# Down-projection weight operands of 5 and 7 of 11 chunk pairs made beside the gate and up products and kept in DRAM

## Chip, cores and metric

The kernel runs on one core of one Trainium2 chip. The metric is the device time of one execution in microseconds; the median of three runs is used. The engines are TensorE (PE), VectorE (DVE), ScalarE (ACT), GpSimd (POOL) and SyncE (SP), which issues all transfers.

## What is computed

Two layers of a decoder trunk on 1024 tokens of 1024 features, in f32. Each has a mixer (three head groups with one input and one output projection) and a feed-forward part; each part is scaled and gated by rows that are made from a condition vector `c`:

```python
for l in range(DEPTH):                       # DEPTH = 2
    mod = (c_act @ ada_w[l] + ada_b[l])[:, None, :]
    sh1, sc1, g1, sh2, sc2, g2 = jnp.split(mod, N_MOD, axis=-1)
    ...                                      # mixer, x = x + g1 * (y @ w_out[l])
    h = rms_norm(x, norm2_w[l]) * (1.0 + sc2) + sh2
    gate, up = jnp.split(h @ w_gate_up[l], 2, axis=-1)
    x = x + g2 * ((jax.nn.silu(gate) * up) @ w_down[l])
return rms_norm(x, final_norm_w)
```

The hidden size of the feed-forward part is 2816: 22 chunks of 128, taken as 11 pairs.

## The kernel before

**Products.** Every f32 product is three matmuls on values split in a high and a low part (`mm3`, lines 132 to 134: high x high, low x high, high x low in some order). `split` (lines 139 to 141) makes the parts: ScalarE casts the high part (L140), VectorE subtracts it from the source for the low part (L137, in the helper `sub`). Gate, up and down products use Winograd's form of Strassen's identity: seven block products in place of eight. The generators `left` and `right` give the operands of the seven products in order, with additions and subtractions of blocks in between, on the engine that their caller names.

**Stages of the feed-forward part.** First the gate and up products, pair by pair (`gu_pair`, `pair_steps`, 11 pairs, 7 products each of 24 matmuls). Their weights are loaded as `gur` (four loads of 0.5 MB a pair), combined on POOL (L1406) and split into `gus`. ScalarE and VectorE take the results out of PSUM (the tiles p1, u2, u4, s12; copies at L1477, L1491, L1496); the activated pairs go to DRAM as `act`. In layer 0 the rows of modulation for later are made beside it (`ada_bg`: one load `ada` of 0.5 MB and one VectorE multiply-add, L254, per product).

Then the down products. The 11 pairs are in four groups (`GROUPS`: pairs 0 to 2, 3 and 4, 5 to 7, 8 to 10). `dn_load` reads the activations (`act`) and the down weights (`dnr`, two tiles of 128x1024 a pair). `dn_prep` multiplies the weights by the gate row g2 (`g2row`, L1531; one tile on VectorE, `GE0`, the other on POOL, `GE1`), builds the left operands from the activations and the right ones from the weights, both with four additions or subtractions of 128x512 on POOL (`DNE`, L1406), and splits both: `dns` (left) and `dnt` (right). `dn_group` makes the seven products of a group: 4 token tiles x 3 (or 2) pairs x 3 matmuls each, and after each token tile VectorE adds the PSUM bank to the residual x (L1556).

**What sets the order.** The program is written as steps; the framework's scheduler then gives each engine one fixed order, which the engine runs through without overtaking. `ahead` in `pair_steps` runs one step of the background work per product and makes operands up to `AHEAD` products ahead; in the down stage `want_dn(7 * gi + i + 2)` makes operands one product ahead of the running one. Buffers are of 4 KB a partition: pool G (`NG` = 30), pool W (`NW` = 12: gus, dns, dnt, ada and the sums acc), pool R (4: gur and the first pair of a group), AD (`NAD` = 3 of 2 KB: differences). A tile waits until the buffer that it takes is released. All transfers stand in one order on SP.

Of the kernel before, what the change touches and what calls it, by code (L numbers as in the profile page):

```python
# [68 lines left out]
NG = 30  # L69
# [3 lines left out]
NAD = 3  # L73
# [3 lines left out]
def tile_trunk(ctx, tc, x, c, positions, ada_w, ada_b, norm1_w, w_in, a_sinks, b_q_norm_w, b_w_uq,  # L77
# [19 lines left out]
    def psum_banks(singles, pairs):  # L97
        """open the PSUM pools of a phase: single banks, and pairs of banks."""
# [77 lines left out]
    # ---- silu(c), features on partitions  # L176
# [17 lines left out]
    def sequences(seqs):  # L194
        """named sequences of steps: run one step of a sequence, or as many as are needed."""
# [25 lines left out]
    # layer 0: the first norm's shift and scale as columns, summed over features by VectorE and TensorE,  # L221
    # applied to normalised tokens that are transposed already
# [34 lines left out]
    def load_ada0(hf):  # L257
        """column half of the rows of shift and scale, loads in the order of use."""
# [41 lines left out]
    def after(dst, src):  # L300
        """the load into dst starts once src is there."""
        DVE.tensor_copy(out=dst[0:1, 0:1], in_=src[0:1, 0:1])

    def setup_rest(late):
        # ---- per-feature vectors: rows in, one transpose, columns out
# [21 lines left out]
        # ---- rotary tables, token-major  # L327
# [23 lines left out]
    def rope(q, nh, half, t, f0):  # L351
        """q: view [P, nh, 2, half] in SBUF, rotated in place."""
# [9 lines left out]
    # ---- adaLN modulation  # L362
# [8 lines left out]
    GE1 = POOL  # L371
    cqd = [[dr.tile([P, 384], F32, name=f"cq{l}_{t}") for t in range(NT)] for l in range(DEPTH)]
# [22 lines left out]
    def ada_rows_wide(l, js):  # L395
        """the same with whole rows at a time, loads one step ahead; five steps per row."""
# [32 lines left out]
    def ada_bg(todo):  # L429
        """the same beside the feed-forward layer, rows (layer, index); nine steps per row."""  # L430
# [27 lines left out]
    # ---- building blocks  # L458
    def transpose_tile(xn):
        """two views [P, 4, P] in PSUM: features on partitions."""  # L460
# [8 lines left out]
    def load_in_chunk(l, c0, n, per, late=None):  # L469
        """in-projection weights [1024, n] at column c0: per-k (hi, lo); generator, fills its list."""  # L470
# [53 lines left out]
    def group_rstd(sq, n, dst):  # L524
        """1/rms over 384 features on partitions; sq(k, i): squares of k-th 128 features, tokens i."""
# [8 lines left out]
    def layer(l, x_tiles):  # L534
# [10 lines left out]
        # -- in-projection: a_v | c_q first, then q | k beside the window attention, c_kv | k_rope, u | v  # L545
# [93 lines left out]
        if l == 0:  # L639
            # the steps of the start, in the order of PRS; each first runs the steps that it needs.  The norm and the  # L640
# [521 lines left out]
        def b_av(h, Q, prs, sm):  # L1162
# [53 lines left out]

            return gen_t(), gen_m()

        # -- output projection, gate folded into its weights
        X = {}  # L1220
        yT = {}

# [498 lines left out]
```

## Time and profile before

| | us |
|---|---|
| median of 3 runs | 2422.22 (2413.93 to 2423.72) |
| span of the profiled execution, first to last instruction | 2416.1 |
| TensorE busy in it | 2270.5 |
| VectorE busy in it | 1783.5 |
| ScalarE busy in it | 1096.1 |
| POOL busy in it | 1088.8 |

The time of the profiled execution as a whole is not among the three runs; only its span is known. TensorE's busy time counts matmuls that are pipelined, so it says when TensorE had work, not how fast it went; the number of matmuls that start in a stretch says that. The rows below are of that execution. "dnt<-dnr" names the written and the read tile without buffer numbers; SPq is SP's order of transfers.

### The profile page before, as it was taken

The page shows a single profiled execution, that of the slowest core. Times are in us where ns is not written, and L with a number is a line of the kernel's source. Part 1 is how long each engine was busy: PE and PEld are TensorE (multiplying, and loading weights), DVE is VectorE, ACT ScalarE, POOL GpSimd, SP SyncE. Part 2 cuts the span into 40 slices and gives each one's busy share as a digit, 9 for nine tenths or more (in the row PEclk, how much of TensorE's full clock was granted, in tenths as well). Part 3 has the DMA queues.
Part 4 walks back from the last instruction along what each step waited for, and adds up shares of the span by engine and source line. Part 5 has one row for each costly group of instructions (what it writes and reads, how often), then busy time and mean ns, then how long its engine had stood idle before and what let it go on. Part 6 is the DMA issues. An engine that isn't in the chain of part 4 may idle for free. (4 is left out here: it accounts for less than half of the span.)

```text
span 2416.1 us, 31750 instructions
## 1 busy us (share of the span) xinstructions
PE 2270.5 (94%) x11195; PEld 1909.4 (79%) x11195; DVE 1783.5 (74%) x2743; ACT 1096.1 (45%) x2244; POOL 1088.8 (45%) x1055
## 2 busy tenths in 40 slices
PE   5999899998999999888899999999899999999897
PEld 4789798887888888776778889888788888887676
DVE  7786678769676667999974854886784444489998
ACT  4566478535333333333344654772553333333333
POOL 4766630243323233856644655112543231375764
PEclk9999999999999999999999999999999999999999
DMA  6403522313454546630140032133223222273111
GB/s 250 163 19 124 169 94 97 127 53 106 156 183 143 167 149 227 225 114 32 32 155 22 21 111 105 53 106 114 78 75 101 79 79 93 69 284 143 36 35 70
DMA packets 133859, 269.01 MB, mean 111 GB/s; under 512 B 10154, under 2 KB 69316, under 8 KB 133700
## 3 DMA queue, kind: packets, MB, share of 16 engines
q1 hardware_dynamic: 133700, 266.99, 32.4%
q8 instruction: 88, 1.44, 0.2%
q14 instruction: 71, 0.58, 0.1%
HBM read 212.38 MB, written 54.57 MB: 110 GB/s over the span
## 5 line engine op out<-in xcount | busy, mean ns | idle before, releaser
L137 DVE TENSOR_TENSOR gus<-gur,gus 128x512 fp32r<-128x512 f32 x264 | 237.9, 914 | 134.4 <-ACT gus L140 133.2
L1406 POOL TENSOR_TENSOR gur<-gur 128x512 f32<-128x512 f32 x44 | 64.1, 1456 | 501.9 <-DVE gus L137 500.9
L140 ACT CAST gus<-gur 128x512 fp32r<-128x512 f32 x264 | 162.4, 622 | 279.0 <-PE gate L134 105.6
L132 PE MATMUL down<-dnt,dns 128*128 128x512 f32 x616 | 248.8, 404 | 38.2 <-DVE x L1556 33.6
L133 PE MATMUL down<-dnt,dns 128*128 128x512 f32 x616 | 248.4, 403 | 15.4 <-DVE dnt L137 15.4
L134 PE MATMUL down<-dnt,dns 128*128 128x512 f32 x616 | 246.4, 400 | 0.0
L133 PE MATMUL gate<-hTl,gus 128*128 128x512 f32 x616 | 240.3, 390 | 4.0 <-DVE hTl L137 4.0
L132 PE MATMUL gate<-hTh,gus 128*128 128x512 f32 x616 | 241.6, 392 | 2.5 <-ACT u L1496 1.3
L132 PE MATMUL up<-hTh,gus 128*128 128x512 f32 x616 | 241.5, 392 | 2.1 <-ACT u L1491 2.1
L134 PE MATMUL up<-hTh,gus 128*128 128x512 f32 x616 | 241.0, 391 | 0.0
L133 PE MATMUL up<-hTl,gus 128*128 128x512 f32 x616 | 241.0, 391 | 0.0
L134 PE MATMUL gate<-hTh,gus 128*128 128x512 f32 x616 | 239.9, 389 | 0.0
L140 ACT CAST dns<-act 128x512 fp32r<-128x512 f32 x132 | 81.7, 619 | 256.3 <-PE down L134 184.6
L132 PEld LDWEIGHTS down<-dnt,dns 128*128 128x128 f32 x616 | 120.3, 195 | 67.7 <-issue 29.1
L133 PEld LDWEIGHTS down<-dnt,dns 128*128 128x128 f32 x616 | 120.5, 196 | 45.1 <-DVE dnt L137 20.1
L1556 DVE TENSOR_TENSOR x<-x,down 128x512 f32<-128x512 f32 x224 | 146.6, 675 | 6.6 <-PE down L134 6.6
L137 DVE TENSOR_TENSOR dnt<-dnr,dnt 128x512 fp32r<-128x512 f32 x132 | 149.7, 1134 | 1.7 <-ACT dnt L140 1.6
L137 DVE TENSOR_TENSOR dns<-act,dns 128x512 fp32r<-128x512 f32 x132 | 136.8, 1036 | 6.8 <-ACT dns L140 6.5
L134 PEld LDWEIGHTS down<-dnt,dns 128*128 128x128 f32 x616 | 120.1, 195 | 25.5
L133 PEld LDWEIGHTS gate<-hTl,gus 128*128 128x128 f32 x616 | 115.8, 188 | 29.0 <-DVE hTl L137 5.6
L132 PEld LDWEIGHTS gate<-hTh,gus 128*128 128x128 f32 x616 | 115.6, 188 | 28.5 <-ACT u L1496 1.7
L132 PEld LDWEIGHTS up<-hTh,gus 128*128 128x128 f32 x616 | 116.8, 190 | 26.7 <-ACT u L1491 2.5
(400 smaller groups left out, 6192.3 us busy)
## 6 DMA issues: line engine op xcount, KB each, us to landing
gur<-in_w_gate_up_dram SPq DMA_DIRECT2D x88, 512.0 KB
ada<-in_ada_w_dram SPq DMA_DIRECT2D x80, 512.0 KB
act<-act SPq DMA_DIRECT2D x44, 512.0 KB
dnr<-in_w_down_dram SPq DMA_DIRECT2D x44, 512.0 KB
wr<-in_w_in_dram SPq DMA_DIRECT2D x24, 512.0 KB
act<-u SPq DMA_DIRECT2D x44, 256.0 KB
x<-in_x_dram SPq DMA_DIRECT2D x16, 512.0 KB
ada0w<-in_ada_w_dram SPq DMA_DIRECT2D x16, 512.0 KB
```

What stands on the lines that cost most here:

```text
L132: PE.matmul(ps, lh, rh, start=start, stop=False, skip_group_check=more)
L133: PE.matmul(ps, lh, rl, start=False, stop=False, skip_group_check=more)
L134: PE.matmul(ps, ll, rh, start=False, stop=stop, skip_group_check=more)
L137: eng.tensor_tensor(out=out_, in0=a, in1=b, op=ALU.subtract)
L140: ACT.copy(out=h, in_=src)
L1406: return lambda o, a, b, op: eng.tensor_tensor(out=o, in0=a, in1=b, op=op)
L1556: DVE.tensor_tensor(out=av_, in0=av_, in1=ps[t], op=ALU.add)
```

## The change

Some pairs are early: 0, 1, 3, 5, 8 in layer 0 and 0, 1, 3, 5, 6, 8, 9 in layer 1. For these the right operands of the down products (weights times g2, the four subtractions, the seven splits) are made by a second background generator, `wd_early`, one step per gate and up product from the second pair on, after 10 steps in layer 0 and 1 in layer 1. Eight steps make a pair. The subtractions are on VectorE there, the multiplication on VectorE and POOL as before. The seven operands of a pair take turns in pool W (`wpe`) and are written to DRAM (`wpd`, 0.5 MB each). In the down stage `dn_prep` reads them back into `dnt` for early pairs, in place of weights, multiplication, subtractions and splits; the left operands are made as before. The row g2 is loaded once, early. NG becomes 33, NAD 4, and a scratch size given to the compiler is made smaller. Comments that the new file leaves out are not shown.

```diff
+EARLY = ((0, 1, 3, 5, 8), (0, 1, 3, 5, 6, 8, 9))
+EARLY0 = (10, 1)
-NG = 30
+NG = 33
-NAD = 3
+NAD = 4
...
+    wpd = [{j: [dr.tile([P, 2, 512], F32, name=f"wp{l}_{j}_{i}") for i in range(7)] for j in EARLY[l]}
+           for l in range(DEPTH)]
...
         def dn_load(grp):
             for j in grp:
                 A = R if j == grp[0] else G
-                r.append([f(2 * j + m, A) for f in (load_act, load_wd) for m in range(2)])
+                r.append((j, [f(2 * j + m, A) for f in ((load_act,) if j in EARLY[l] else (load_act, load_wd))
+                              for m in range(2)]))
...
+        def wd_early():
+            for _ in range(EARLY0[l]):
+                yield
+            g2.append(mod_row(l, 5))
+            for j in EARLY[l]:
+                ws = [load_wd(2 * j + m, G) for m in range(2)]
+                yield
+                for w, E in zip(ws, (GE0, GE1)):
+                    E.tensor_tensor(out=w, in0=w, in1=g2[0], op=ALU.mult)
+                last = None
+                for i, src in enumerate(right(ws[0][:, :512], ws[0][:, 512:], ws[1][:, :512], ws[1][:, 512:],
+                                              AD("t2"), tt_on(DVE))):
+                    v = W([P, 2, 512], F32R, "wpe")
+                    split(src, v[:, 0], v[:, 1])
+                    if last is not None:
+                        DMA.dma_start(out=wpd[l][j][i - 1], in_=f32(last))
+                    last = v
+                    if i < 6:
+                        yield
+                yield
+                DMA.dma_start(out=wpd[l][j][6], in_=f32(last))
...
         def dn_prep(raws):
...
-            for _ in range(7):
+            for i in range(7):
                 ops = []
-                for gl, gr in gens:
+                for j, gl, gr in gens:
+                    v = W([P, 2, 512], F32R, "dnt")
+                    if gr is None:
+                        DMA.dma_start(out=f32(v), in_=wpd[l][j][i])
                     w = W([P, 2, 512], F32R, "dns")
                     split(next(gl), w[:, 0], w[:, 1])
-                    v = W([P, 2, 512], F32R, "dnt")
-                    split(next(gr), v[:, 0], v[:, 1])
+                    if gr is not None:
+                        split(next(gr), v[:, 0], v[:, 1])
...
                 if j > 0:
                     run(bg)
+                    run(bg2)
...
+        bg2 = wd_early()
         for j in range(1, NJ):
             drain(pair_steps(j))
         drain(bg)
+        drain(bg2)
...
-        g2row = mod_row(l, 5)
...
-    nc = _bacc.Bacc("TRN2", target_bir_lowering=False, num_devices=1)
+    nc = _bacc.Bacc("TRN2", target_bir_lowering=False, num_devices=1, dynamic_dma_scratch_size=1024)
```

TensorE's order is the same in both kernels. On the other engines it shows at three places. The first is VectorE in the last group (pairs 8 to 10) of layer 0's down stage, one product. Before:

```order
L1556 TENSOR_TENSOR x_9452<-x_9452,down_10778 128x512
L1556 TENSOR_TENSOR x_9454<-x_9454,down_10779 128x512
L1556 TENSOR_TENSOR x_9456<-x_9456,down_10780 128x512
L137 TENSOR_TENSOR dns_11040<-act_10368,dns_11040 128x512
L137 TENSOR_TENSOR dnt_11044<-dnr_10372,dnt_11044 128x512
L1556 TENSOR_TENSOR x_9458<-x_9458,down_10781 128x512
L137 TENSOR_TENSOR dns_11047<-act_10376,dns_11047 128x512
L137 TENSOR_TENSOR dnt_11051<-dnr_10380,dnt_11051 128x512
L137 TENSOR_TENSOR dns_11054<-act_10384,dns_11054 128x512
L137 TENSOR_TENSOR dnt_11058<-dnr_10388,dnt_11058 128x512
```

And after the change:

```order
L1590 TENSOR_TENSOR x_9723<-x_9723,down_10977 128x512
L1590 TENSOR_TENSOR x_9725<-x_9725,down_10978 128x512
L1590 TENSOR_TENSOR x_9727<-x_9727,down_10979 128x512
L139 TENSOR_TENSOR dns_11294<-act_10584,dns_11294 128x512
L139 TENSOR_TENSOR dns_11298<-act_10588,dns_11298 128x512
L1590 TENSOR_TENSOR x_9729<-x_9729,down_10980 128x512
L139 TENSOR_TENSOR dnt_11297<-dnr_10592,dnt_11297 128x512
L139 TENSOR_TENSOR dns_11305<-act_10596,dns_11305 128x512
L139 TENSOR_TENSOR dnt_11304<-dnr_10600,dnt_11304 128x512
```

One subtraction of ten operations is gone, that of the early pair 8. The second place is SP's order of transfers in layer 0's gate and up stage, around the loads `gur` of the sixth pair. Before:

```order
L1472 DMA act_7_222<-u_1512_7268 128x512
L1426 DMA gur_7508<-in_w_gate_up_dram 128x4x256
L1426 DMA gur_7510<-in_w_gate_up_dram 128x4x256
L435 DMA ada_7505<-in_ada_w_dram 128x1024
L1426 DMA gur_7512<-in_w_gate_up_dram 128x4x256
L1426 DMA gur_7514<-in_w_gate_up_dram 128x4x256
L1472 DMA act_8_223<-p_1524_7386 128x512
```

And after the change (`wp_1_3` is the fourth operand of pair 1 in DRAM):

```order
L1476 DMA act_7_222<-u_1523_7392 128x512
L439 DMA ada_7612<-in_ada_w_dram 128x1024
L1550 DMA wp_1_3_269<-wpe_7577 128x1024
L1550 DMA wp_1_4_270<-wpe_7615 128x1024
L1430 DMA gur_7666<-in_w_gate_up_dram 128x4x256
L439 DMA ada_7659<-in_ada_w_dram 128x1024
L1430 DMA gur_7668<-in_w_gate_up_dram 128x4x256
L1430 DMA gur_7670<-in_w_gate_up_dram 128x4x256
L1476 DMA act_8_223<-p_1540_7525 128x512
L1430 DMA gur_7672<-in_w_gate_up_dram 128x4x256
L1550 DMA wp_1_5_271<-wpe_7662 128x1024
L1516 DMA dnr_7775<-in_w_down_dram 128x1024
```

Three stores and a load of down weights stand between and behind the gate loads. The third place is ScalarE at the same point of the program. Before:

```order
L140 CAST gus_7527<-gur_7512 128x512
L140 CAST gus_7530<-gur_7510 128x512
L140 CAST gus_7533<-gur_7514 128x512
L1491 COPY u_1555_7568<-gate_7387 128x512
L140 CAST gus_7538<-gur_7508 128x512
L1491 COPY u_1556_7570<-up_7388 128x512
```

And after the change:

```order
L142 CAST wpe_7662<-dnr_7413 128x512
L142 CAST gus_7674<-gur_7334 128x512
L142 CAST gus_7677<-gur_7338 128x512
L142 CAST gus_7682<-gur_7666 128x512
L142 CAST gus_7685<-gur_7670 128x512
L142 CAST gus_7688<-gur_7668 128x512
L1495 COPY u_1575_7726<-gate_7526 128x512
L142 CAST gus_7691<-gur_7672 128x512
L142 CAST gus_7696<-gur_7666 128x512
L1495 COPY u_1576_7728<-up_7527 128x512
```

The cast of an early operand has come in ahead, and a cast of `gus` has moved from before the first copy of `u` to behind it, where it takes the buffer that the store wp_1_5 releases.

## Rows read from the trace of the kernel before

**Rows 1.** Page, part 1: busy us, share of the span, instructions.

```profile
PE 2270.5 (94%) x11195; PEld 1909.4 (79%) x11195; DVE 1783.5 (74%) x2743; ACT 1096.1 (45%) x2244; POOL 1088.8 (45%) x1055
```

**Rows 2.** Tile down, each layer: ns min/median/max, first to last start in us.

```profile
L132 PE MATMUL down<-dnt,dns x308: 387/389/767, 984.2 to 1234.2; 128*128 128x512 f32 x154
...
L132 PE MATMUL down<-dnt,dns x308: 387/389/793, 2160.4 to 2406.3; 128*128 128x512 f32 x154
```

**Rows 3.** Timeline of PE, layer 0's down stage, first and last of 42 rows: start, us.

```profile
1140.66 0.39 PE L132 MATMUL down<-dnt,dns 128*128 128x512 f32 x1
...
1149.95 0.39 PE L134 MATMUL down<-dnt,dns 128*128 128x512 f32 x1
```

**Rows 4.** Windows of ten us, layer 0's down stage; x counts what started.

```profile
core 0: us, PE busy (x) PEld busy (x) DVE busy (x) ACT busy (x) POOL busy (x), PEclk, DMA share, GB/s
...
994.00:1004.00 10.00, 8.73 (x39) 6.94 (x38) 10.00 (x9) 2.75 (x5) 9.92 (x7) 1.00 1.00 391
1004.00:1014.00 10.00, 7.86 (x34) 5.89 (x33) 10.00 (x8) 4.37 (x8) 9.92 (x5) 1.00 0.60 240
1014.00:1024.00 10.00, 7.59 (x22) 5.63 (x22) 10.00 (x12) 0.00 (x0) 1.88 (x1) 0.66 0.12 43
1024.00:1034.00 10.00, 10.00 (x46) 8.26 (x45) 10.00 (x16) 3.72 (x7) 1.83 (x1) 1.00 0.75 274
...
1114.00:1124.00 10.00, 6.23 (x28) 4.82 (x26) 10.00 (x9) 3.74 (x7) 10.00 (x7) 1.00 0.00 1
...
1134.00:1144.00 10.00, 10.00 (x46) 8.29 (x45) 8.86 (x15) 4.97 (x10) 0.00 (x0) 1.00 0.35 107
```

**Rows 5.** Waits of PE in layer 0's down stage: us in total, times, longest.

```profile
PE down L132 <- DVE x L1556: 16.8, 4, 6.0
PE down L133 <- DVE dnt L137: 10.9, 7, 2.4
```

**Rows 6.** Timeline of POOL and DVE, layer 0's down stage: start, us, operation.

```profile
1007.48 8.39 POOL L1531 TENSOR_TENSOR dnr<-dnr,mrow 128x1024 f32<-128x1024 f32 x3
...
1010.79 2.87 DVE L137 TENSOR_TENSOR dnt<-t,dnt 128x512 fp32r<-128x512 f32 x1
...
1022.22 0.68 DVE L137 TENSOR_TENSOR dnt<-dnr,dnt 128x512 fp32r<-128x512 f32 x1
```

**Rows 7.** Groups by line, layer 0's down stage: busy us, mean ns, idle before.

```profile
L137 DVE TENSOR_TENSOR dnt<-dnr,dnt 128x512 fp32r<-128x512 f32 x62 | 69.1, 1115 | 0.0
L1531 DVE TENSOR_TENSOR dnr<-dnr,mrow 128x1024 f32<-128x1024 f32 x8 | 13.3, 1668 | 0.0
...
L1406 POOL TENSOR_TENSOR t<-dnr,dnr 128x512 f32<-128x512 f32 x11 | 19.0, 1731 | 0.0
...
L140 ACT CAST dnt<-dnr 128x512 fp32r<-128x512 f32 x61 | 37.6, 617 | 20.5 <-POOL dnr L1406 17.7 <-DVE dnr L1531 2.8
```

**Rows 8.** Windows in the gate and up stages of layers 0 and 1, columns as rows 4.

```profile
650.00:860.00 210.00, 210.00 (x945) 173.93 (x944) 138.01 (x171) 76.13 (x134) 68.81 (x46) 1.00 0.48 155
1780.00:2100.00 320.00, 320.00 (x1414) 264.96 (x1413) 158.22 (x211) 119.41 (x205) 105.25 (x72) 1.00 0.27 88
```

**Rows 9.** Groups by line of DVE, layer 0's gate and up stage, 650 to 860.

```profile
L137 DVE TENSOR_TENSOR gus<-gur,gus 128x512 fp32r<-128x512 f32 x64 | 57.2, 908 | 31.7 <-ACT gus L140 31.3
L254 DVE SCALAR_TENSOR_TENSOR acc<-ada,cact,acc 128x1024 f32<-128x1024 f32 x27 | 34.6, 1282 | 16.1 <-DMA ada<-in_ada_w_dram 16.0
```

**Rows 10.** Waits in the gate and up stages: PE layer 0, PE layer 1, ACT layer 0.

```profile
PE up L132 <- ACT u L1491: 2.1, 1, 2.1
...
PE gate L132 <- ACT u L1496: 1.3, 1, 1.3
...
ACT gus L140 <- DVE acc L254: 30.9, 15, 4.7
```

**Rows 11.** Chain of waits around layer 1's down stage: start, us, what.

```profile
2125.58 5.20 DMA dnr<-in_w_down_dram
...
2137.93 4.98 DMA act<-act
...
2159.72 7.47 DMA dnr<-in_w_down_dram
```

More of the change, by code (lines that the diff above doesn't have):

```diff
@@ L1523, in dn_load @@
                 A = R if j == grp[0] else G
-                r.append([f(2 * j + m, A) for f in (load_act, load_wd) for m in range(2)])
-            return r
+                r.append((j, [f(2 * j + m, A) for f in ((load_act,) if j in EARLY[l] else (load_act, load_wd))
+                              for m in range(2)]))
+            return r
+        g2 = []
+        def wd_early():
[19 more added lines that the diff above has]
+                DMA.dma_start(out=wpd[l][j][6], in_=f32(last))
@@ L1527, in dn_prep @@
         def dn_prep(raws):
             gens = []
-            for a0, a1, w0_, w1_ in raws:
-                for w, E in ((w0_, GE0), (w1_, GE1)):
-                    E.tensor_tensor(out=w, in0=w, in1=g2row, op=ALU.mult)
-                gens.append((left(a0[:, 0, :], a1[:, 0, :], a0[:, 1, :], a1[:, 1, :], SM([P, 512], F32, "s2"), tt_on(DNE)),
-                             right(w0_[:, :512], w0_[:, 512:], w1_[:, :512], w1_[:, 512:], AD("t2"), tt_on(DNE))))
-            for _ in range(7):
+            for j, (a0, a1, *ws) in raws:
+                for w, E in zip(ws, (GE0, GE1)):
+                    E.tensor_tensor(out=w, in0=w, in1=g2[0], op=ALU.mult)
+                gens.append((j, left(a0[:, 0, :], a1[:, 0, :], a0[:, 1, :], a1[:, 1, :], SM([P, 512], F32, "s2"), tt_on(DNE)),
+                             right(ws[0][:, :512], ws[0][:, 512:], ws[1][:, :512], ws[1][:, 512:], AD("t2"), tt_on(DNE))
+                             if ws else None))
```

## The prediction

> **What bounds the kernel now.** I read the busy times of the engines first, then the stretches of the two down projections, then what sits idle there and why. TensorE is busy 94% of a span of 2416.1 us and VectorE 74% [rows 1], so time can be won only where TensorE waits. The down products of the two layers run from 984.2 to 1234.2 us and from 2160.4 to 2406.3 us [rows 2]: 250.0 and 245.9 us from the first of 308 triples to the last, that is over 922 paces (924 matmuls). An unhindered matmul of this stage starts 0.2266 us after the one before (41 paces in 9.29 us [rows 3]), so 922 of them need 208.9 us. The stage loses **41.1 us in layer 0 and 37.0 us in layer 1, 78.1 us in all**.
>
> Where is it lost? In windows of ten us [rows 4], TensorE starts 46 matmuls wherever POOL is mostly idle, and 34, 22 or 28 at the end of a stretch in which POOL is busy; VectorE is busy all the time there; the granted clock falls to 0.66 in the window with 22, which is part of the loss. What changes is how many operations VectorE completes: 15 or 16 in ten us with POOL idle, 8 or 9 with POOL at 9.9 or 10.0. A subtraction takes 0.68 us alone and 2.87 us beside the multiplication of POOL (three in 8.39 us) [rows 6]. TensorE's waits are for the sums into x and for the low halves dnt [rows 5], both VectorE's. So VectorE sets the pace while POOL prepares a group, and TensorE does in the rest.
>
> One product of a group of three pairs has 36 matmuls, 36 x 0.2266 = 8.16 us, and asks VectorE for six subtractions and four sums. Ten operations at 9 in ten us take 11.1 us, at 15 in ten us 6.7 us. POOL's busy stretch per group: per pair one multiplication (2.80 us, rows 6) and about five subtractions before the third and fourth products can be made (1.73 us each [rows 7]), 11.4 us; three pairs 34 us. Loss per group 34 x (1 - 8.16/11.1) = 9.0 us; for the group of two pairs (eight operations, 8.9 us, against 5.44 us; stretch 22.8 us) 8.9 us. Sum 35.9 us a layer, against 41.1 and 37.0 measured: 39.05 on average, so I scale the model by 1.09.
>
> **The change, part by part.** *Down stage, work taken out.* For an early pair VectorE loses its multiplication (1.67 us) and seven subtractions dnt (1.1 us each [rows 7]), ScalarE seven casts, and POOL one multiplication and four subtractions, three of them in the busy stretch. The order of the last group of layer 0 shows it: ten VectorE operations per product become nine. TensorE's order is the same in both kernels. With one early pair of three, a product asks for nine operations (10.0 us at the rate beside POOL) and the stretch is 2 x 11.4 + 2 x 1.73 = 26.3 us: loss 26.3 x (1 - 8.16/10.0) = 4.8 us. With two of three: eight operations, 8.9 us, stretch 18.3 us: 1.5 us. With one of two: seven, 7.8 us, stretch 14.9 us: 4.5 us. Layer 0 has groups with 2, 1, 1, 1 early pairs: 1.5 + 4.5 + 4.8 + 4.8 = 15.6 us. Layer 1 has 2, 1, 2, 2: 9.0 us. Scaled: 24.6 x 1.09 = 26.8 us left of 78.1. **Gain 51 us**; what is late next is TensorE itself. Bounds: 78 us if no stall is left, 25 us if the rate beside POOL falls in step with the operations removed, so that only half goes.
>
> The Trainium skill puts a rule to this contention ("SBUF — State Buffer", section "SBUF: two separate sides"): a VectorE operation with two SBUF inputs and a GpSimd operation that reads SBUF exclude each other for a whole instruction. By that rule each subtraction costs one POOL operation (1.73 us) while the sums, which read PSUM, stay at 0.6 us; the same working then gives 93 us of stalls before and 31 after, which scaled to the measured 78.1 leaves 26 us, and the forecast does not move. The 2.87 us beside 2.80 us agrees with it; that eight or nine operations fit in ten us, sums among them, is a little better than it allows.
>
> *Down stage, reads added.* 35 and 49 loads of 0.5 MB. In the order each waits for the buffer of a product two before it in a group of three pairs, whose last quarter frees it, so it is issued 1.19 products or 9.7 us ahead. Loads of this size took 4.98 to 7.47 us [rows 11]: hidden, unless the next group's loads are ahead of them (below). Where these are, the engines are full: 391 GB/s at a share of 1.00 [rows 4]. 3 MB ahead of the third product of a group is 8 us: I take one us for each layer, **2 us**; bounds 0 and the first rival.
>
> *Gate and up stage, work added.* Per early pair VectorE gets one multiplication (1.67 us), four subtractions (taken from POOL) and seven low halves, at the 0.91 us that such an operation has in this stage [rows 9]: 1.67 + 11 x 0.91 = 11.7 us. It is spread over eight products, 8 x 24 x 0.2266 = 43.5 us, so 27% of VectorE. VectorE is busy 138.01 of 210 us in layer 0 and 158.22 of 320 us in layer 1 [rows 8], 66% and 49%, which become 93% and 76%. ScalarE gets seven casts of 0.62 us [rows 7], 10% on its 36%. POOL gets nothing but what it does now. TensorE is busy all of the time in both windows, and its longest waits in the two stages are 2.1 and 1.3 us [rows 10], although ScalarE already waits up to 4.7 us behind VectorE for a buffer: operands lie ahead by products. At 93% some of it will show: I take one wait of the size seen, 1.7 us, in each of the six gate pairs of layer 0 that carry added work, **10 us**, and nothing in layer 1. Bounds: 0, and the slower rival. Nothing excludes a loss here; a gain is excluded, since TensorE has nothing to win.
>
> *DMA in that stage.* Per early pair 1 MB is read and 3.5 MB written, 4.7 MB in 43.5 us or 108 GB/s on 155 GB/s (share 0.48) in layer 0 and on 88 (0.27) in layer 1 [rows 8]. At 391 GB/s for a full share that is 0.28 more: 0.76 and 0.55. It fits, but loads of ada, for which VectorE already waits 16.1 us in 210 [rows 9], will land later; this is in the 10 us. The buffers NG, NAD cost nothing on the chip; attention code is reordered a little (no price in the trace, taken as 0, bounds -5 and 5).
>
> Sum: -51 + 2 + 10 = **-39 us**. The span was 2416.1 us; the profiled run's own time is not among the three given (2413.93 to 2423.72), whose median lies 6.1 us above the span. 2422 - 39 = **2383 us**, a span near 2377.
>
> **Rivals.** *A, the reads arrive late.* SP issues in order and the loads of the next group stand between the reads of products two to four. If in each of the eight groups three products wait 1.5 us for their reads, 36 us go and 2419 us remain. For: share 1.00 in the first ten us of the stage. Against: POOL's and VectorE's release of buffers spreads those loads.
>
> *B, slower.* ScalarE casts in order. In layer 0's fifth pair the cast gus_7691 takes a buffer from a wpe whose store stands behind four gate loads on SP, and the copy u_1576 that TensorE waits for stands two casts later. TensorE has 12 matmuls, 2.7 us, of slack at such a copy, and a buffer is taken again some 1.5 products (8.2 us) after its cast, so a store that lands within 10.9 us costs nothing; each us beyond costs 84 us over 84 stores. Landing at 11.7 us costs 67 us in place of the 10: 2440 us. For: 2 MB of loads ahead at 391 GB/s are 5.4 us on top of 7.47 us [rows 11]. Against: only one or two of seven stores stand there. No row shows when a store has landed. The Trainium skill ("DMA: Bandwidth & Descriptors", "Anatomy of one DMA — SWDGE (gpsimd) path") says that completion waits for a receipt and can be surprisingly late when the target is HBM, which speaks for B; its fit for another queue, 2.0 us plus bytes at 436 GB/s, gives as an estimate 3.2 us for 0.5 MB, which speaks against it.
>
> *C, better.* Gate and up hide all, and stalls shrink to under 10 us: 2422 - 68 = 2354 us. For: ScalarE's 4.7 us waits do not reach TensorE today.
>
> *D, no effect*, since some other wait of the stage (the sums' 16.8 us at group starts) is not VectorE's backlog: 2422 us.
>
> **How the numbers follow.** Forecast (2366 to 2400) 0.60, A 0.12, B 0.12, C 0.11, D 0.05. About 0.5% or 12 us can be told from no change. Faster: 0.60 + 0.11 + a part of A, 0.75. Same: the rest of A and D, 0.13. Slower: B, 0.12. The range 2352 to 2416 leaves out B, half of A and D, and the best of C, some 0.2.
>
> **What would show it.** Right: no ten-us window of the down stages under 38 matmuls except at a group of two pairs; VectorE below 90% there; waits of TensorE for x and dnt under 10 us a layer, and no more than 5 us for the new reads; VectorE near 93% in layer 0's gate stage with TensorE still over 97%. Wrong: TensorE waiting for DMA dnt (A); ScalarE's casts waiting for wp stores and TensorE for its copies u (B); matmul counts as before although VectorE has gaps (D).

## The result, and the profile after

The changed kernel takes **2388.5 us** (2387.2 to 2390.4, four runs); the kernel before took 2419.9 us (2413.9 to 2423.7) beside it. The ratio is 0.9876, interval 0.9859 to 0.9894: 31 us faster; 39 were forecast. The profiled execution has a span of 2386.4 us, 29.7 us less than before. The page's busy times, to be read against [rows 1]:

```profile
PE 2260.2 (95%) x11195; PEld 1901.0 (80%) x11195; DVE 1798.0 (75%) x2791; ACT 1097.9 (46%) x2244; POOL 1007.6 (42%) x1007
```

POOL gave up 81 us and VectorE gained 15. Where the time went is read from the first starts of the tiles `gate` and `down`, which bound the stages. For the down products (one of three matmuls, tile view of each layer: ns min/median/max, first to last start; compare [rows 2]):

```profile
L134 PE MATMUL down<-dnt,dns x308: 389/389/636, 1005.8 to 1229.6; 128*128 128x512 f32 x154
...
L134 PE MATMUL down<-dnt,dns x308: 389/389/501, 2165.4 to 2377.7; 128*128 128x512 f32 x154
```

223.8 and 212.3 us, where 250.0 and 245.9 stood: the down stages won **59.8 us**. The same starts, and those of `gate`, give all stages. Here a down stage ends with the last start of any of its matmuls, hence a few tenths more:

| us | gate, up L0 | down L0 | mixer L1 | gate, up L1 | down L1 | span |
|---|---|---|---|---|---|---|
| before | 449.5 | 250.5 | 487.1 | 438.6 | 246.3 | 2416.1 |
| after | 471.0 | 224.2 | 484.4 | 451.0 | 212.8 | 2386.4 |
| difference | +21.5 | -26.3 | -2.7 | +12.4 | -33.5 | -29.7 |

The gate and up stages gave **33.9 us** back.

**Down stage.** Windows of ten us, layer 0 (x counts what started; compare [rows 4]):

```profile
core 0: us, PE busy (x) PEld busy (x) DVE busy (x) ACT busy (x) POOL busy (x), PEclk, DMA share, GB/s
...
1020.00:1030.00 10.00, 5.88 (x23) 3.57 (x22) 9.41 (x9) 2.39 (x4) 7.59 (x4) 1.00 1.03 415
...
1080.00:1090.00 10.00, 7.06 (x23) 4.88 (x23) 10.00 (x11) 1.76 (x3) 8.58 (x4) 0.83 0.15 52
...
1110.00:1120.00 10.00, 10.00 (x46) 8.29 (x45) 10.00 (x12) 2.19 (x4) 9.84 (x7) 1.00 0.05 20
...
1170.00:1180.00 10.00, 10.00 (x46) 8.28 (x45) 10.00 (x10) 4.41 (x8) 10.00 (x7) 1.00 0.23 66
1180.00:1190.00 10.00, 8.45 (x38) 6.72 (x37) 10.00 (x11) 4.12 (x8) 10.00 (x8) 1.00 0.26 91
```

POOL still works in bursts and VectorE is still full in them, but TensorE now starts 46 matmuls beside a full POOL in most of them. Two deep dips are left in layer 0: the second is in the group of two pairs, the first in the first group, where the DMA engines are full with reads. What TensorE waits for in this stage (us in total, times, longest; compare [rows 5]):

```profile
PE down L134 <- issue: 2.8, 1, 2.8
PE down L135 <- DVE dnt L139: 2.6, 1, 2.6
PE down L134 <- ACT dnt L142: 2.4, 2, 1.5
PE down L134 <- DMA dnt<-wp: 1.2, 2, 1.0
...
PE down L134 <- DVE x L1590: 0.2, 1, 0.2
```

"issue" means that the view shows nothing that TensorE waited for. By the times it was a sum into x on VectorE: the 2.8 us end at 1083.67 us, 0.1 us after such a sum (1082.89 us, 0.68 us long). Layer 1's only stop over 0.2 us, one of 2.5 us in the window from 2180 us, ends the same way at 2184.42 us, after the first of three sums from 2183.65 us. Ahead of these stands a subtraction beside POOL's multiplication:

```profile
2180.35 2.82 POOL L1561 TENSOR_TENSOR dnr<-dnr,mrow 128x1024 f32<-128x1024 f32 x1
```

```profile
2180.86 2.86 DVE L139 TENSOR_TENSOR dnt<-dnr,dnt 128x512 fp32r<-128x512 f32 x1
```

So the 16.8 us for x and 10.9 us for dnt in layer 0 are 3.0, with that stop, and 2.6. What is left is mostly still VectorE beside POOL; the reads are 1.2 us.

**Gate and up stage.** The same stretch, 640 to 960 us, in the kernel before (first) and after:

```profile
640.00:960.00 320.00, 320.00 (x1435) 264.71 (x1435) 213.05 (x265) 115.31 (x204) 96.83 (x66) 1.00 0.51 165
```

```profile
640.00:960.00 320.00, 303.40 (x1325) 246.23 (x1324) 250.21 (x301) 123.42 (x224) 109.27 (x69) 0.98 0.64 217
1780.00:2100.00 320.00, 309.45 (x1354) 255.32 (x1353) 235.08 (x284) 142.46 (x249) 120.10 (x72) 0.98 0.54 191
```

In layer 0, 110 of 1435 matmuls are missing: 110 x 0.2266 = 25 us. TensorE is idle for 16.6 us of them; a mean granted clock of 0.98 over 320 us accounts for some 6 more, by an estimate from two digits. TensorE waits mostly for ScalarE's copies out of PSUM (compare [rows 10]):

```profile
PE up L134 <- ACT u L1495: 5.3, 3, 2.7
PE up L134 <- ACT u L1500: 4.5, 3, 2.2
```

Ten-us windows show where:

```profile
690.00:700.00 10.00, 7.33 (x34) 5.78 (x34) 4.88 (x7) 3.93 (x8) 4.42 (x4) 0.95 0.95 333
700.00:710.00 10.00, 6.92 (x20) 5.16 (x19) 9.88 (x11) 2.67 (x5) 9.61 (x6) 0.71 0.02 9
...
730.00:740.00 10.00, 10.00 (x46) 8.29 (x45) 7.18 (x12) 4.20 (x8) 1.11 (x1) 1.00 0.88 251
740.00:750.00 10.00, 7.98 (x34) 5.91 (x34) 7.96 (x6) 3.41 (x7) 8.50 (x6) 1.00 0.60 211
...
820.00:830.00 10.00, 8.98 (x42) 6.86 (x40) 9.18 (x14) 3.63 (x7) 3.48 (x3) 1.00 0.98 327
830.00:840.00 10.00, 7.28 (x29) 5.60 (x30) 8.76 (x7) 4.34 (x9) 9.92 (x6) 0.95 0.05 18
```

The dips come once a pair: first a window with the DMA engines nearly full (the loads `gur` of the next pair, which the stores and the loads `ada` and `dnr` now share them with), then POOL's burst on `gur`, in which VectorE completes 6, 7 or 11 operations, where the windows from 730 and 820 us have 12 and 14. Inside one of them, the timelines of POOL, VectorE and ScalarE (start, us, operation, idle time before and what ended it):

```profile
746.27 2.59 POOL L1543 TENSOR_TENSOR dnr<-dnr,mrow 128x1024 f32<-128x1024 f32 x1 [1.34 <-DMA dnr<-in_w_down_dram]
748.82 3.42 POOL L1410 TENSOR_TENSOR s<-gur,gur 128x512 f32<-128x512 f32 x2
```

```profile
746.53 4.58 DVE L139 TENSOR_TENSOR gus<-gur,gus 128x512 fp32r<-128x512 f32 x2
751.03 0.67 DVE L1502 TENSOR_TENSOR u<-u,gate 128x512 f32<-128x512 f32 x1
```

```profile
743.82 1.14 ACT L142 CAST gus<-gur 128x512 fp32r<-128x512 f32 x2 [3.03 <-DMA wp<-wpe]
744.86 0.58 ACT L1495 COPY u<-up 128x512 f32<-128x512 f32 x1
...
751.74 0.63 ACT L1474 ACTIVATE u<-u 128x512 f32<-128x512 f32 x1 [5.29 <-DVE u L1502]
752.28 0.57 ACT L1500 COPY u<-up 128x512 f32<-128x512 f32 x1
```

Two subtractions take 4.58 us beside POOL, the addition into u waits behind them, ScalarE's activation waits 5.29 us for it, and the copy of the next PSUM bank (752.28 us) waits behind that: TensorE stops for 1.7 us. POOL's multiplication there is early work too; before the change it stood in the down stage. Just before, a cast had waited 3.03 us for a store to land, with the copy at 744.86 us behind it: a second way to a stop, of 1.6 us. A third is a late gate load, here ahead of the copy that TensorE waited 2.67 us for:

```profile
696.65 1.14 ACT L142 CAST gus<-gur 128x512 fp32r<-128x512 f32 x2 [4.70 <-DMA gur<-in_w_gate_up_dram]
```

Sorted by what stands ahead of the operation that TensorE waited for, the 16.6 us are 8.7 us behind VectorE's backlog (six stops), 5.6 behind late loads `gur` (four), 1.6 behind the store and 0.6 behind a load `ada`.

In layer 1 the loss is one event, at the first early pair, 1780 to 1820 us. VectorE's and ScalarE's timelines there:

```profile
1786.14 1.23 DVE L1543 TENSOR_TENSOR dnr<-dnr,mrow 128x1024 f32<-128x1024 f32 x1 [7.32 <-DMA dnr<-in_w_down_dram]
```

```profile
1787.40 0.62 ACT L142 CAST wpe<-dnr 128x512 fp32r<-128x512 f32 x1 [10.13 <-DVE dnr L1543]
...
1802.28 1.14 ACT L142 CAST gus<-gur 128x512 fp32r<-128x512 f32 x2 [6.02 <-DMA gur<-in_w_gate_up_dram]
```

The multiplication of the first weights, loaded one product ahead, holds VectorE for 7.32 us; the cast behind it holds ScalarE for 10.13 us; the buffers of `gur` come free late, the next loads land late, and TensorE stops for 3.3 and 7.2 us, the longer of them here:

```profile
PE up L134 <- ACT u L1495: 7.2, 1, 7.2
```

### The profile page after: what moved, and what is told of

It reads as the page before. It is cut to its first block, busy times and chain, and to the rows that moved or that the text cites. A ratio compares the mean times of both kernels' runs of the same rounds, so it can differ in the third digit from the quotient of the medians.

```text
span 2386.4 us, 32032 instructions
## 1 busy us (share of the span) xinstructions
PE 2260.2 (95%) x11195; PEld 1901.0 (80%) x11195; DVE 1798.0 (75%) x2791; ACT 1097.9 (46%) x2244; POOL 1007.6 (42%) x1007
## 5 line engine op out<-in xcount | busy, mean ns | idle before, releaser
L139 DVE TENSOR_TENSOR gus<-gur,gus 128x512 fp32r<-128x512 f32 x264 | 264.9, 1026 | 78.2 <-ACT gus L142 77.1
L134 PE MATMUL up<-hTh,gus 128*128 128x512 f32 x616 | 244.7, 397 | 16.9 <-ACT u L1495 12.5
L134 PE MATMUL down<-dnt,dns 128*128 128x512 f32 x616 | 241.8, 392 | 9.3 <-issue 5.3
L135 PE MATMUL down<-dnt,dns 128*128 128x512 f32 x616 | 241.1, 391 | 2.6 <-DVE dnt L139 2.6
L136 PE MATMUL up<-hTh,gus 128*128 128x512 f32 x616 | 242.7, 394 | 0.0
L136 PE MATMUL down<-dnt,dns 128*128 128x512 f32 x616 | 241.2, 392 | 0.3 <-DVE dns L139 0.3
L134 PEld LDWEIGHTS up<-hTh,gus 128*128 128x128 f32 x616 | 117.7, 191 | 45.2 <-ACT u L1495 14.4
L139 DVE TENSOR_TENSOR dns<-act,dns 128x512 fp32r<-128x512 f32 x132 | 134.8, 1038 | 16.3 <-ACT dns L142 16.2
L134 PEld LDWEIGHTS down<-dnt,dns 128*128 128x128 f32 x616 | 116.3, 189 | 37.0 <-issue 6.6
L135 PEld LDWEIGHTS down<-dnt,dns 128*128 128x128 f32 x616 | 116.4, 189 | 26.9 <-DVE dnt L139 3.1
L136 PEld LDWEIGHTS up<-hTh,gus 128*128 128x128 f32 x616 | 117.6, 191 | 25.0
L135 PEld LDWEIGHTS up<-hTl,gus 128*128 128x128 f32 x616 | 117.8, 191 | 24.1
```

Of the source, the lines that this page charges most:

```text
L134: PE.matmul(ps, lh, rh, start=start, stop=False, skip_group_check=more)
L135: PE.matmul(ps, lh, rl, start=False, stop=False, skip_group_check=more)
L136: PE.matmul(ps, ll, rh, start=False, stop=stop, skip_group_check=more)
L139: eng.tensor_tensor(out=out_, in0=a, in1=b, op=ALU.subtract)
```

## Experiments

Stage times of all kernels, read as above (L0, L1: layers; time: median; ratio to the kernel before, with its interval). They are of one profiled execution each, which took 5.9 us more than its kernel's median in e8, 5.9 us less in e12, and was within 3 us in the others; the same code gave gate and up stages up to 3.5 us apart.

| kernel | gate, up L0 | down L0 | gate, up L1 | down L1 | time | ratio |
|---|---|---|---|---|---|---|
| after | 471.0 | 224.2 | 451.0 | 212.8 | 2388.5 | 0.9876 [0.9859, 0.9894] |
| e1 layer 1 only | 451.5 | 248.8 | 450.8 | 212.8 | 2391.8 | 0.9888 [0.9869, 0.9908] |
| e2 layer 0 only | 469.3 | 225.6 | 437.2 | 248.2 | 2409.3 | 0.9961 [0.9948, 0.9974] |
| e3 one store in seven | 461.9 | 224.7 | 450.0 | 212.8 | 2379.0 | 0.9832 [0.9816, 0.9849] |
| e4 weights loaded early | 479.7 | 224.2 | 438.2 | 214.1 | 2384.3 | 0.9856 [0.9836, 0.9876] |
| e5 early operands in pool G | 482.6 | 224.3 | 464.7 | 214.2 | 2412.8 | 0.9974 [0.9958, 0.9990] |
| e6 begun four steps later | 476.8 | 225.3 | 442.8 | 214.4 | 2383.9 | 0.9850 [0.9830, 0.9870] |
| e7 e5 in L0, e4 in L1 | 478.3 | 224.5 | 441.7 | 212.8 | 2385.1 | 0.9866 [0.9841, 0.9890] |
| e8 no arithmetic | 460.1 | 225.2 | 446.8 | 214.4 | 2371.0 | 0.9806 [0.9786, 0.9825] |
| e9 no work of POOL on gur | 449.6 | 224.5 | 440.5 | 213.0 | 2352.6 | 0.9728 [0.9713, 0.9742] |
| e10 e3 and e8 | 449.2 | 225.5 | 446.0 | 214.5 | 2365.3 | 0.9772 [0.9754, 0.9791] |
| e11 e4 in L1 alone | 468.6 | 224.5 | 441.7 | 214.1 | 2377.8 | 0.9828 [0.9812, 0.9845] |
| e12 e11, gur on VectorE | 460.8 | 224.1 | 436.0 | 212.8 | 2365.3 | 0.9783 [0.9760, 0.9806] |

The down stages are the same in every kernel that has the layer's early pairs, within 2 us. All that the runs move is in the gate and up stages.

**The layers apart, e1 and e2.**

```diff
-EARLY = ((0, 1, 3, 5, 8), (0, 1, 3, 5, 6, 8, 9))
+EARLY = ((), (0, 1, 3, 5, 6, 8, 9))      (e1)
+EARLY = ((0, 1, 3, 5, 8), ())            (e2)
```

> Only layer 1 keeps early pairs. Theory P (the two layers' gains and costs add up, as read off the changed kernel's trace: layer 0 wins 26.2 us in the down stage and loses 21.5 in the gate and up stage, so its early pairs are worth 4.7): layer 0's gate and up stage near 449 us and its down stage near 250 as before the change, layer 1's as after (451, 212); time 2388.5 + 4.7 = 2393. Rival R (layer 0's early pairs are worth what the prediction said, about 13 us net, and the trace of one execution misleads): 2401 or more.

> Only layer 0 keeps early pairs. Theory P: layer 1 loses its net of 33.6 - 12.4 = 21.2 us, with its gate and up stage back to 439 and its down stage to 246 us; time 2388.5 + 21 = 2410. Rival R: the 12.4 us that layer 1's gate and up stage lost come from layer 0's stage that precedes it (order of buffers), not from layer 1's own early pairs: that stage stays at 450 and the time is 2420.

2391.8 and 2409.3 us, as theory P said. Costs and gains belong to the layer's own early pairs. Layer 0's are worth 3 us on top of layer 1's (2391.8 to 2388.5) and 9 us alone (e2 against the kernel before, interval 6 to 13 us); the trace gave 4.7. So most of what they win in the down stage (25 us) they lose before it.

**The stores, e3.**

```diff
-                    if last is not None:
-                        DMA.dma_start(out=wpd[l][j][i - 1], in_=f32(last))
                     last = v
...
-                        DMA.dma_start(out=f32(v), in_=wpd[l][j][i])
+                        DMA.dma_start(out=f32(v), in_=wpd[l][j][6])
```

> The early operands are made as in the changed kernel, but only the seventh of each pair is stored; the reads, as many and as large as before, all take that one (the down products get wrong right operands for early pairs). 30 of 35 and 42 of 49 stores are gone. Theory S (the stores cost the gate and up stages: their place in SP's order, their traffic beside the loads gur and ada, and the buffers that they hold): layer 0's stage falls from 471 to about 455 us, layer 1's from 451 to about 445, waits of ScalarE for wp vanish and those for gur shrink by half; time about 2367. Theory V (VectorE's added work and the weights that come one step ahead of their use cost it): both stages stay within 4 us of 471 and 451; time 2382 to 2390.

Between the two: layer 0's stage falls by 9.1 us, layer 1's by 1.0. The stores cost something in layer 0, where the rows `ada` are loaded beside them, and nothing that can be told in layer 1. By which way is not shown: the halving of ScalarE's waits for `gur` that theory S expected did not come (38.3 us, against 37.9 after the change, from 530 to 1000 us).

**The first weights of layer 1, e4, e6, e11.**

```diff
-            for j in EARLY[l]:
-                ws = [load_wd(2 * j + m, G) for m in range(2)]
+            nxt = [load_wd(2 * EARLY[l][0] + m, G) for m in range(2)]
+            for _ in range(4):
+                yield
+            for n, j in enumerate(EARLY[l]):
+                ws = nxt
                 yield
...
                     last = v
+                    if i == 3 and n + 1 < len(EARLY[l]):
+                        nxt = [load_wd(2 * EARLY[l][n + 1] + m, G) for m in range(2)]
```

> The weights of the first early pair of each layer are loaded five steps ahead of the multiplication in place of one, those of every later pair about four steps ahead. Theory V: the wait of VectorE for the first weights in layer 1 (7.3 us) and what hangs on it (gus subtractions, loads gur, two stops of TensorE of 3.4 and 7.2 us) are gone: layer 1's gate and up stage falls from 451 to about 441 us, layer 0's by 0 to 5 us; time 2374 to 2379. Theory S: the weights' wait only uncovers a queue that is too full, and the stage stays within 4 us: 2385 to 2392.

Layer 1's stage is at 438.2 us: its whole cost is gone. But layer 0's rose by 8.7 us, which neither theory said, so the time falls by 4 us only. e4 also begins the work four steps later, which e6 does alone (`EARLY0 = (14, 5)`):

> Early work begins four steps later in both layers, with the weights loaded one step ahead as in the changed kernel. It tells what of the run with the weights loaded earlier was the lead and what was the shift. Theory L (lead): layer 1's gate and up stage stays near 451 us, layer 0's near 471; time 2386 to 2391. Rival F (the shift): layer 1's stage falls to about 438 and layer 0's rises to about 480 us, as in that run; time 2380 to 2386.

The rival F is mostly right: 442.8 and 476.8 us. Of layer 1's 12.8 us the later beginning alone gives 8.2, and of layer 0's loss of 8.7 it makes 5.8. e11 leaves layer 0 as in the changed kernel and takes e4's loads in layer 1 alone:

> The changed kernel with layer 1's first early weights loaded five steps ahead and the later ones four, layer 0 as it is. If layer 1's gain of 12.8 us is that of the loads and of the later start in layer 1 alone: its gate and up stage near 438 us, layer 0's near 471; time 2374 to 2378, the best kernel so far. If part of it came from layer 0's different state: 442 or more; 2379 to 2385.

2377.8 us: 10.7 us better than the changed kernel, 9.3 of them in layer 1's stage and the rest not told apart. The time is as expected; the stage, 441.7 us, is at the edge of the rival's. That stage has the same code in e4, e7 and e11 and took 438.2, 441.7 and 441.7 us, so the share of the loads beside that of the later beginning is known to some 3 us only. What is shown: the cost in layer 1 hangs on where the first pair begins and how late its weights are, not on the amount of added work. POOL's sums take part in it, as e9 shows below.

**Buffers, e5 and e7: a theory that fell.** ScalarE's casts of `gus` wait for buffers of pool W; I supposed that the early operands take them.

```diff
-                    v = W([P, 2, 512], F32R, "wpe")
+                    v = G([P, 2, 512], F32R, "wpe")      (e5; in e7 for layer 0 alone, and e4's loads in layer 1)
```

> The early operands take their buffers from pool G in place of pool W, from which gus, ada and acc take theirs; nothing else changes. Theory W (in layer 0's gate and up stage the early operands and their unlanded stores hold buffers that gus needs, so gate and up operands lie fewer products ahead and every late load or subtraction reaches TensorE): layer 0's stage falls from 471 to 452 to 459 us, ScalarE's waits for wp and for acc shrink to under a third; layer 1's stays near 451 since its loss is one event; time about 2372 to 2378. Theory V (VectorE has too much to do there): layer 0's stage stays between 466 and 471 us; time 2384 to 2389.

> Layer 0's early operands in pool G as in the first of these runs; layer 1's in pool W with the weights loaded five and four steps ahead. If both causes are as theories W and L say and add up: layer 0's stage 452 to 459, layer 1's near 438 us, down stages near 224 and 214; time about 2360 to 2366. If W is wrong and L right: 2374 to 2378. If both are wrong: 2386.

Both theories missed: in e5 both stages got longer, by 11.6 and 13.7 us. e7 has layer 1's gain (441.7 us) and the loss in layer 0 (478.3). The windows of e5:

```profile
640.00:960.00 320.00, 293.15 (x1274) 238.03 (x1273) 250.46 (x294) 120.33 (x217) 109.77 (x66) 0.97 0.63 215
1780.00:2100.00 320.00, 300.31 (x1299) 244.65 (x1298) 247.89 (x276) 135.21 (x240) 129.06 (x76) 0.99 0.52 183
```

VectorE is as busy as after the change in layer 0 and 13 us busier in layer 1, and completes fewer operations (294 for 301, 276 for 284). Why was not settled: the scheduler's order changes as well. Theory W fell, since moving the early operands out of pool W does not help. That buffers do not matter is not shown: from 530 to 1000 us ScalarE's casts of `gus` wait 65.2 us for buffers that the sums acc release, against 41.0 after the change.

**VectorE's work and POOL's bursts, e8 to e10.** e8 splits the raw weights:

```diff
-                for w, E in zip(ws, (GE0, GE1)):
-                    E.tensor_tensor(out=w, in0=w, in1=g2[0], op=ALU.mult)
-                for i, src in enumerate(right(ws[0][:, :512], ws[0][:, 512:], ws[1][:, :512], ws[1][:, 512:],
-                                              AD("t2"), tt_on(DVE))):
+                for i in range(7):
+                    src = ws[i % 2][:, 512 * (i % 4 // 2):512 * (i % 4 // 2) + 512]
```

> Early operands are split and stored as before, but of the raw weights: the multiplication by the gate row and the four subtractions of each early pair are left out (the down products of early pairs get wrong right operands). VectorE loses 1.67 + 4 x 0.9 = 5.3 of the 11.7 us that a pair adds, POOL its multiplication. Theory V: layer 0's gate and up stage falls from 471 to about 459 us or less and layer 1's from 451 to about 445; time 2370 or less. Theory W with L: layer 0's stage stays above 465 us; layer 1's falls only if the cast no longer waits long for the weights, which are still one step ahead: above 445; time 2378 to 2388.

460.1 us in layer 0: 10.9 us belong to five operations of VectorE (and one of POOL) in each pair, near theory V. Layer 1's stage falls by 4.2 us. e10 has both omissions:

> Both omissions of earlier runs at once: one store in seven, and early operands split from raw weights without multiplication and subtractions (values of early pairs wrong). Alone they took layer 0's gate and up stage from 471.0 to 461.9 and to 460.1 us. If they are two separate causes: 451 us, within 2 of the 449.5 before the change, and time about 2361 to 2366. If both remove the same thing (one coupling of late loads and a busy VectorE): 458 to 461, time about 2368 to 2371.

449.2 us, that is the 449.5 of before: the two are separate causes, 9.1 and 10.9 us one by one, and together they make up the 21.5. From 640 to 960 us 40 matmuls come back in e3, 49 in e8 and 95 of the 110 in e10. By the times the sum is rougher, 9.5 and 17.5 us one by one and 23.2 together. e9 asks whether VectorE's part is its amount of work or the company of POOL:

```diff
-                gens.append(left(r0[:, :, 0, :], r1[:, :, 0, :], r0[:, :, 1, :], r1[:, :, 1, :], tmp, tt_on(POOL)))
+                a11, a12, a21, a22 = r0[:, :, 0, :], r1[:, :, 0, :], r0[:, :, 1, :], r1[:, :, 1, :]
+                gens.append(iter((a11, a12, a11, a22, a21, a12, a22)))
```

> The changed kernel, but POOL's eight additions and subtractions on the gate and up weights of each pair are left out in both layers (the left operands of the gate and up products are the raw blocks, so the values are wrong); traffic, stores, casts and VectorE's work stay. Theory C (VectorE is slowed to a half while POOL works, as in the down stage, so the work that the change gave VectorE cannot be done inside POOL's bursts, and TensorE's stops fall into these): layer 0's gate and up stage falls from 471 to 450 to 457 us. Theory S (loads gur and ada land late behind the added traffic, whatever the engines do): it stays at 464 us or above. Layer 1's stage falls below 446 under C only if its late start matters less without the bursts; down stages 224 and 213. Time: C 2360 to 2375, S 2378 or more.

```profile
640.00:960.00 320.00, 312.33 (x1390) 255.60 (x1390) 229.90 (x314) 128.12 (x231) 12.82 (x5) 1.00 0.68 232
```

The stage is back at 449.6 us with all the added work in it, as theory C said, and the time is even below C's range. But pairs without early work have less to do too, also outside the window, so the window says more: 65 of the 110 missing matmuls are back, 15 of 25 us. The other 45 remain, with a DMA share of 0.68; they are taken to be the stores' part, which no run tests together with e9. An operation of VectorE takes 229.90/314 = 0.73 us there, against 0.83 after the change.

Leaving out POOL's sums also shortens the way from a load to its operands, a rival to the company of POOL. Against it: in layer 0's stage of the changed kernel ScalarE's casts wait only 2.3 us for POOL's sums, while its waits for VectorE's sums into u (L1502) fall from 30.0 us to 16.4 in e9 and 16.2 in e12.

Layer 1's stage falls to 440.5 us although the first weights are as late as before (VectorE waits 6.71 us for them). TensorE loses 34 matmuls at that event (27 and 31 start in the ten us from 1760 and 1770) in place of 62 (26, 8 and 42 from 1790 in the changed kernel): POOL's bursts make up nearly half of it.

**The same sums on VectorE, e12.** If an operation of POOL costs VectorE more than the operation itself would, VectorE should do it.

```diff
-                gens.append(left(r0[:, :, 0, :], r1[:, :, 0, :], r0[:, :, 1, :], r1[:, :, 1, :], tmp, tt_on(POOL)))
+                gens.append(left(r0[:, :, 0, :], r1[:, :, 0, :], r0[:, :, 1, :], r1[:, :, 1, :], tmp, tt_on(DVE)))
```

> As the run before it (layer 1's weights loaded ahead), and the eight additions and subtractions on the gate and up weights of each pair are on VectorE in place of POOL, in both layers. Theory C (POOL's bursts halve VectorE, so an operation costs VectorE more when POOL does it than when it does it itself): from 640 to 960 us VectorE gets 64 operations more of some 0.68 us, 44 us, and its 301 others lose the 0.10 us that they took longer than without the bursts (0.83 against 0.73 us), 30 us: 264 of 320 us busy against 250; no more bursts, so layer 0's gate and up stage falls from 468.6 to between 452 and 462 us and layer 1's stays near 440; time 2362 to 2374. Rival V (it is VectorE's amount of work and its order that hold the rest up, bursts or not): VectorE has more to do and stops at each late load gur, layer 0's stage rises to 475 us or more, layer 1's to 446 or more; time 2385 or more.

```profile
640.00:960.00 320.00, 309.85 (x1371) 252.96 (x1371) 262.72 (x373) 127.17 (x229) 13.23 (x5) 0.99 0.67 224
1780.00:2100.00 320.00, 320.00 (x1413) 265.00 (x1412) 232.86 (x356) 146.01 (x252) 14.38 (x6) 1.00 0.52 184
```

2365.3 us (2359.4 to 2369.1), and VectorE's 262.72 us against the 264 worked out ahead. Layer 1's stretch in e11, which differs in the sums alone:

```profile
1780.00:2100.00 320.00, 317.91 (x1403) 262.90 (x1402) 231.51 (x287) 142.34 (x249) 127.82 (x79) 1.00 0.54 190
```

There VectorE does 356 operations in place of 287 and is busy for 232.86 us in place of 231.51: the 69 more cost it next to nothing. Layer 0's stage falls from 468.6 to 460.8 us, layer 1's from 441.7 to 436.0. This kernel computes all that the changed one does and is 23 us faster than it, 54 us faster than the one before. Layer 1's stage is now shorter than the 438.6 us before the change, so a part of this gain may have been there to take without the change; that was not tried.

The Trainium skill ("SBUF — State Buffer", section "SBUF: two separate sides") calls the port pair that VectorE and GpSimd share an exclusive lock: of a VectorE operation with two SBUF inputs and a GpSimd operation that reads SBUF, one blocks the other for the whole instruction. The runs are in line with it, though none shows the lock itself: a subtraction of `gus` has a mean of 1.031 us from 640 to 960 us after the change and 0.755 us in e12:

```profile
L139 DVE TENSOR_TENSOR gus<-gur,gus 128x512 fp32r<-128x512 f32 x92 | 92.5, 1031 | 29.1 <-ACT gus L142 28.7
```

```profile
L139 DVE TENSOR_TENSOR gus<-gur,gus 128x512 fp32r<-128x512 f32 x92 | 67.5, 755 | 24.6 <-ACT gus L142 24.5
```

## Why the prediction was right or wrong

*Down stage, the bound and the work taken out:* right, and a little too small. That VectorE beside POOL sets the pace, and that 78.1 us can be won, is borne out by the waits that vanished. 14.9 and 3.4 us of stalls are left, 18.3 in all; 26.8 were forecast, and 2 for the reads. The term that was mis-sized is VectorE's rate beside POOL, nine operations in ten us: with fewer subtractions of dnt among them, 10 to 12 fit (windows from 1110 and 1170). So 59.8 us were won and not 49. (Between the starts that were read lie 921 paces, not 922; that is 0.2 us a layer.)

*Reads:* right in size, TensorE waits 1.2 us for them. They show where rival A put them, in the first group with the DMA engines full (share 1.03), and only there; rival A's price did not come.

*Gate and up stage:* here the prediction failed, 33.9 us against 10. Three steps of it were wrong. The first is the price: 0.91 us was taken for each added operation and the average share of 93% was asked whether it fits. In the same stretch VectorE came to 170.31 of 210 us, 81%, and still TensorE stopped:

```profile
650.00:860.00 210.00, 194.63 (x839) 157.09 (x839) 170.31 (x203) 80.15 (x146) 71.06 (x43) 0.98 0.69 237
```

The bursts of POOL decide: an operation of VectorE takes 7.96/6 = 1.3 us in the window from 740 us and 7.18/12 = 0.6 us in that from 730. That mechanism was the prediction's own for the down stage; it was not carried to this one. The second is "POOL gets nothing but what it does now": in this stage POOL got the multiplication of the second weight tile, 2.59 us in the burst shown above, and its busy time from 640 to 960 us rose from 96.83 to 109.27 us. VectorE's groups from 650 to 860 us, to be read with [rows 9], show who pays:

```profile
L139 DVE TENSOR_TENSOR gus<-gur,gus 128x512 fp32r<-128x512 f32 x55 | 56.4, 1052 | 17.6 <-ACT gus L142 17.3
...
L139 DVE TENSOR_TENSOR wpe<-dnr,wpe 128x512 fp32r<-128x512 f32 x26 | 18.4, 712 | 1.6 <-ACT wpe L142 1.2
```

The added low halves cost 0.71 us, less than the price; those of `gus` went from 0.91 to 1.05 us. The third wrong step is "nothing in layer 1", read from a share of 76% (73% was measured): the 12.4 us there are one event, a load that comes one product ahead of its use at the head of an engine's order, made worse by POOL's bursts. The prediction listed the loads but not who is queued behind the multiplication.

*DMA in that stage:* shares of 0.69 and 0.54, forecast 0.76 and 0.55. "It fits" was wrong in layer 0 all the same: 9.1 us belong to the stores (e3). The mean hides windows of 0.88 to 0.98 ahead of the dips, in which `gur` is loaded; that the stores do their harm there is argued, not shown.

*Rival B* had a right place, a cast behind a store's landing (3.03 us at 743.82), but not its price; 2440 us was far off. *C* was right that the stalls of the down stages shrink, wrong on the rest. *D* fell: the waits for the sums went with VectorE's work. Of the signs that were named: TensorE's waits for x and dnt are under 10 us and those for reads under 5, VectorE is at 89.7% and 82% in the down stages; but two ten-us windows under 38 matmuls lie in first groups (23 from 1020 us, 34 from 2180), and TensorE is at 95% in layer 0's gate stage (640 to 960 us), not over 97%, with VectorE at 81%, not 93%.

That the time came out close is luck in part: 11 us too little gain in the one term stood against 24 us too little loss in the other.

What stays open: how the stores cost their 9.1 us. The remaining 11.3 us of layer 0's stage in e12 (460.8 against 449.5) are taken to be the stores, by e10; e12 without stores was not tried. Why layer 0's stage grows by 5.8 us when the early work begins four steps later is not settled either.

## What to carry to other kernels

Price work that is moved beside a busy engine by the windows in which that engine's neighbour is at work, not by its mean: a mean share of 81% hid bursts in which VectorE's operations took twice as long, and about half of layer 0's 21 us went there. Where VectorE and POOL both work on blocks in SBUF, an operation put on POOL is no relief once VectorE has work in the same moment; moving eight sums a pair from POOL to VectorE took some 12 us off (2377.8 to 2365.3). And a new load needs its lead from the engine that will stand at it in order: at the head of VectorE's order one late load of weights held up three engines for 7 to 10 us each.

## What the runs showed of the hardware

The stops of TensorE cost more than their length. Two stops of the changed kernel:

```profile
698.32 0.50 PE L134 MATMUL up<-hTh,gus 128*128 128x512 f32 x1 [2.67 <-ACT u L1495]
706.01 0.38 PE L387 MATMUL mcT<-ident,mc 128*8 128x128 f32 x1 [3.08 <-DVE mc L383]
```

The granted clock of 700 to 710 us was 0.71 (a part of the window at the lower of the two levels, 1.2 and 2.4 GHz), with 20 matmuls started where 46 are usual; some 6 of the 25 us that the stretch lost are clock, by the estimate above. In e9, where no stop from 640 to 960 us is longer than 1.73 us, every window of that stretch has 1.00.

With three loads into 0.5 MB each issued within 1.3 us (the row g2 and two tiles of weights, 1779.3 to 1780.6 us, layer 1), the multiplication of the first weights began at 1786.14 us, 6.4 us after the first of these tiles was issued. The fit that the prediction quoted from the Trainium skill ("DMA: Bandwidth & Descriptors", "Anatomy of one DMA — SWDGE (gpsimd) path") is for another queue and gives 3.2 us for one of them as an estimate; in company it took about twice that here.
